# Conditioning shift and scale for the first block: the weighted sum over 1024 inputs on TensorE instead of VectorE

## The chip, the cores and the metric

One core of one Trainium2 chip runs the whole kernel. The metric is device time in microseconds (us), from start to end of one execution. TensorE (PE in the profile; PEld is its weight load, LDWEIGHTS) multiplies a stationary block of up to 128 columns with a moving operand and writes into PSUM. VectorE (DVE), ScalarE (ACT) and GpSimd (POOL) do the elementwise work, and SyncE (SP) issues the DMA transfers.

## What is computed

A decoder layer on 2048 tokens of width 1024. What matters here is its very first part: a vector `c` is put through SiLU and projected to six vectors of 1024; the first two, a shift and a scale, act on the normalised input before its projection.

```python
x = layer_norm(x, ln_in_g, ln_in_b)
c_act = jax.nn.silu(c)
mod = c_act @ w_ada[l] + b_ada[l]
sh1, sc1, gt1, sh2, sc2, gt2 = [m[:, None, :] for m in jnp.split(mod, 6, axis=-1)]
h = x * (1.0 + sc1) + sh1
proj = h @ w_in[l]
```

Behind this stand attention in a low-rank form, a retention mixer, the output projection and a squared-ReLU MLP, all in float32, with the large products computed as three products of split operands.

## The kernel before

The tokens are worked in four blocks of 512 (four tiles of 128 tokens). In the first stage, `ln_in` loads a tile of x (L259) and normalises it: statistics on DVE (L187 to L198) with two small steps on POOL (L179, L180), then the scaling on ACT (L262). `make_h` transposes the normalised tiles on TensorE so that features lie on partitions (L276, eight feature blocks k, four transposes each), applies scale and shift while it takes them out of PSUM (ACT, L280), splits the result in a high and a low part (L124, L126, L127) and stores it for a later stage (L283). `in_proj_mm` then does the first input projection, 416 columns wide, with three matmuls for each pair of token tile and k (L130 to L132, tiles `pa`), 96 for a block.

The shift and scale that L280 needs come from `w_ada`, a matrix of 1024 by 2048 for these two vectors (8 MB). The loop over g at L309 takes it in four groups; group g gives the features of blocks k = 2g and 2g + 1. For each group eight tiles of 128 x 2 x 256 are loaded (L313, tiles `wada`, 256 KB each, 21 buffers under the tag `wt`, later used for other weights too). `cact` holds the activated vector, one column for each of the eight input blocks. DVE then multiplies tile 0 by its column (L324) and adds the seven others, each times its column (L326), into the same tile. What is left is a sum over the 128 partitions, done by TensorE: with the bias put into PSUM first (L329, the identity as stationary operand), four matmuls add it up (L332), with a 128-column piece of the accumulated tile stationary and one column of ones moving. Three small DVE steps make the scale `gs1` and the shift `bs1` out of it (L333 to L335). `make_h(0, ...)` for this group and, for g > 0, the projection of the group before it follow (L336 to L341).

The text of the program is not the order of instructions. A scheduler orders each engine's queue at build time by priorities and a simulated timeline; what stands under `tc.high_priority` (L322 to L335) is preferred as soon as it is ready there. Each engine then works through its queue in that order, and SP issues the transfers in a fixed order as well. PSUM tiles of the tag `tp` (four buffers) serve `psX` and the transposes `psT`, and four of the tag `mm` serve `pa`.

Of the kernel before, what the change touches and what calls it, by code (L numbers as in the profile page):

```python
# [14 lines left out]
OP = mybir.AluOpType  # L15
# [3 lines left out]
P = 128  # L19
# [5 lines left out]
KD = D // P  # L25
# [90 lines left out]
def build(nc, tc, I, out, upto=9, dbg=None):  # L116
    dbg = {} if dbg is None else dbg
    V, A, G, T, Q = nc.vector, nc.scalar, nc.gpsimd, nc.tensor, nc.sync
# [39 lines left out]
    def fmc(n):  # L158
        return fm[:, FM[n][0]:FM[n][1]]
# [6 lines left out]
    ones = keep.tile([P, P], F32, name="ones")  # L166
# [3 lines left out]
    cact = keep.tile([P, 8], F32, name="cact")  # L170
# [67 lines left out]
    def tables16():  # L238
        a16 = s1.tile([P, NT, 16], F32, tag="ang", name="a16")
        V.tensor_tensor(a16, posf.unsqueeze(2).broadcast_to([P, NT, 16]),  # L240
                        cnc("inv16").unsqueeze(1).broadcast_to([P, NT, 16]), op=OP.mult)
        sincos(s1, a16.rearrange("p a b -> p (a b)"), NT * 16, sin16[:, :, 16:32], cos16[:, :, 0:16], "a16")
        G.tensor_copy(cos16[:, :, 16:32], cos16[:, :, 0:16])
        G.tensor_scalar(sin16[:, :, 0:16], sin16[:, :, 16:32], -1.0, 0.0, op0=OP.mult, op1=OP.add)
# [12 lines left out]
    def ln_in(tt):  # L257
        xt = px.tile([P, D], F32, tag="x", name=f"x{tt}")
        Q.dma_start(xt, I["x"][tt * P:(tt + 1) * P, :])  # L259
        rs, nm = xst[:, tt, 0:1], xst[:, tt, 1:2]  # L260
        ln_stats(sm, xt, rs, nm)
        A.activation(xt, xt, AF.Identity, bias=nm, scale=rs)  # L262
        xts[tt] = xt
# [5 lines left out]
    def make_h(b, ks=range(KD)):  # L269
        if ks[0] == 0:  # L270
            hs[b] = hp.tile([P, 4, KD, P], R32, tag="hh", name=f"hh{b}"), hp.tile([P, 4, KD, P], R32, tag="hl", name=f"hl{b}")
        hh, hl = hs[b]
        for k in ks:
            ps = pst1.tile([P, 4, P], F32, tag="tp", name=f"psT{b}_{k}")
            for t in range(4):
                T.transpose(ps[:, t, :], xts[4 * b + t][:, k * P:(k + 1) * P], ident)  # L276
            if k % 2 == 0:
                h2 = hfp.tile([P, 4, 2, P], F32, tag="hf", name=f"hf{b}_{k}")
            hf = h2[:, :, k % 2]
            A.activation(hf, ps, AF.Identity, bias=bs1[:, k:k + 1], scale=gs1[:, k:k + 1])  # L280
            split(hf, hh[:, :, k, :], hl[:, :, k, :], HH[HHE[b > 0]], HH[HLE[k % len(HLE)]] if b == 0 else V)
            if k % 2 == 1:
                Q.dma_start(h_d[b].rearrange("t p k c -> p t k c")[:, :, k - 1:k + 1], h2)  # L283
# [3 lines left out]
    def in_proj_mm(b, order):  # L287
        hh, hl = hs[b]
        for t, k in order:
            if k == 0:  # L290
                pas[b, t] = ps1.tile([P, 512], F32, tag="mm", name=f"pa{4 * b + t}")
            mm3(pas[b, t][:, 0:NA], hh[:, t, k, :], hl[:, t, k, :], wa_h[:, k, :], wa_l[:, k, :], k == 0, k == KD - 1)
# [8 lines left out]
    def load_wa(ks):  # L301
        for k in ks:
            wt = s0.tile([P, NA], F32, tag="wt3", name=f"wa{k}", bufs=6)
            Q.dma_start(wt, I["w_in_a"][k * P:(k + 1) * P, :])
            split(wt, wa_h[:, k, :], wa_l[:, k, :], A, G)
# [3 lines left out]
    for g in range(4):  # L309
        wts = []  # L310
        for k in range(KD):
            wt = s0.tile([P, 2, 256], F32, tag="wt", name=f"wada{g}_{k}", bufs=WTB)
            Q.dma_start(wt, I["w_ada"][k * P:(k + 1) * P, 0:2 * D].rearrange("p (e c) -> p e c", e=2)  # L313
                        [:, :, g * 256:(g + 1) * 256])
            wts.append(wt)
        if g == 0:
            ln_in(2)
            ln_in(3)
            load_wa(range(0, 4))
        if g == 1:  # L320
            load_wa(range(4, 8))
        with tc.high_priority(offset=HPO):  # L322
            acc = wts[0]
            V.tensor_scalar(acc, acc, cact[:, 0:1], None, op0=OP.mult)  # L324
            for k in range(1, KD):
                V.scalar_tensor_tensor(acc, wts[k], cact[:, k:k + 1], acc, op0=OP.mult, op1=OP.add)  # L326
            psA = pst1.tile([P, 2, 2], F32, tag="tp", name=f"psX{g}")
            fs = slice(2 * g, 2 * g + 2)
            T.matmul(psA, ident, fmc("b_ada")[:, 0:16].rearrange("p (s k) -> p s k", s=2)[:, :, fs], start=True, stop=False)  # L329
            for e in range(2):  # L330
                for f in range(2):
                    T.matmul(psA[:, e, f:f + 1], acc[:, e, f * P:(f + 1) * P], ones[:, 0:1], start=False, stop=e + f == 2)  # L332
            V.scalar_tensor_tensor(gs1[:, fs], psA[:, 1, :], 1.0, fmc("gin")[:, fs], op0=OP.add, op1=OP.mult)  # L333
            V.scalar_tensor_tensor(bs1[:, fs], psA[:, 1, :], 1.0, fmc("bin")[:, fs], op0=OP.add, op1=OP.mult)
            V.tensor_tensor(bs1[:, fs], bs1[:, fs], psA[:, 0, :], op=OP.add)  # L335
        make_h(0, [2 * g, 2 * g + 1])  # L336
        if g > 0:
            in_proj_mm(0, [(t, k) for k in (2 * g - 2, 2 * g - 1) for t in range(4)])
        if g == 0:
            tables16()  # L340
# [3 lines left out]
    for k in range(2):  # L344
        for c0, c1 in ((0, 512), (512, WQ)):
# [4 lines left out]
                                   op0=OP.mult, op1=OP.subtract)  # L350
# [810 lines left out]
    acc = {}  # L1161
# [147 lines left out]
def program(L, upto=9, dbg=None):  # L1309
    import concourse.bacc as bacc  # L1310
    nc = bacc.Bacc("TRN2", target_bir_lowering=False, num_devices=1)
    I = {n: nc.dram_tensor(f"in_{n}", v.shape, mybir.dt.from_np(v.dtype), kind="ExternalInput").ap() for n, v in L.items()}
    out = nc.dram_tensor("out", (S, D), F32, kind="ExternalOutput").ap()
    with tile.TileContext(nc, schedule_with_timeline_sim=True) as tc:
        build(nc, tc, I, out, upto, dbg)
    return nc
# [8 lines left out]
```

## Time and profile before

| | us |
|---|---|
| median of 3 runs (lowest, highest) | 2668.42 (2666.13, 2670.19) |
| the profiled execution | 2668.93 |
| its span, first to last instruction | 2667.2 |
| busy PE, PEld | 2461.4, 2030.5 |
| busy DVE, ACT, POOL | 1895.4, 1061.6, 1155.0 |

The busy time of an engine counts its instructions; overlapping ones are counted once. The granted clock (PEclk) is a share of the full rate of TensorE, 1.00 or 0.50. In the trace of this kernel one matmul call in float32 stands as two LDWEIGHTS and two MATMUL, except for transposes. In a timeline, neighbouring instructions of the same kind are merged, with their count behind an x; what stands in brackets is the engine's idle time before them and what ended it.

### The profile page before, as it was taken

How to read it: one execution, taken by the hardware profiler on the slowest of the kernel's cores; microseconds unless marked ns; L12 is line 12 of the kernel's file. 1: busy time of each engine (PE TensorE's matmuls, PEld its weight loads, DVE VectorE, ACT ScalarE, POOL GpSimd, SP SyncE). 2: the span in 40 equal slices, each digit the busy share in tenths (PEclk: the TensorE clock that was granted, in tenths of full speed). 3: DMA queues.
4: the chain of work that ended last, by engine and by line, in shares of the span. 5: the costliest groups of instructions: out<-in, count | busy, mean ns of one | idle time of the engine just before them, and what ended most of it. 6: DMA issues, size and time to landing. Idle time of an engine off the chain costs nothing.

```text
span 2667.2 us, 33679 instructions
## 1 busy us (share of the span) xinstructions
PE 2461.4 (92%) x11668; PEld 2030.5 (76%) x11668; DVE 1895.4 (71%) x3047; ACT 1061.6 (40%) x2093; POOL 1155.0 (43%) x1055
## 2 busy tenths in 40 slices
PE   6999999989999999999689998799998999999996
PEld 5887878877787878787477786577786888878885
DVE  8757675566767676856898877988765665786657
ACT  4653222256777777434433334233321211221111
POOL 4323545557888888587612335432330000330004
PEclk9999999989999999999799999899998999999998
DMA  9466341020102021556487852677739677676653
GB/s 324 145 208 209 115 131 44 32 75 28 58 23 64 22 60 48 184 183 215 147 265 251 283 180 76 218 255 270 278 102 374 257 257 261 257 282 241 230 192 126
DMA packets 194250, 464.68 MB, mean 174 GB/s; under 512 B 17560, under 2 KB 51736, under 8 KB 179744
## 3 DMA queue, kind: packets, MB, share of 16 engines
q1 hardware_dynamic: 194080, 462.54, 50.0%
q8 instruction: 92, 1.51, 0.2%
q14 instruction: 78, 0.64, 0.1%
HBM read 313.30 MB, written 149.17 MB: 173 GB/s over the span
## 4 chain that ended last, share of the span: by engine, by line
PE 53%; DVE 17%; DMA 13%; issue 7%; POOL 6%; ACT 4%; SPq 1%; DVEq 0%; ACTq 0%; POOLq 0%
PE d_W L130 4%; PE d_W L132 4%; PE d_W L131 4%; DMA wt_d<-w2s 4%; PE t L833 3%; DMA wad<-in_w_ada 2%; PE pj L132 2%; PE pj L131 2%; PE pj L130 2%; PE o L826 2%; PE d_Z L130 2%; PE d_Z L131 2%; PE d_Z L132 2%; DVE w1l_P L127 2%; PE o L824 2%
## 5 line engine op out<-in xcount | busy, mean ns | idle before, releaser
L179 POOL TENSOR_SCALAR rs<-mv 128x1 f32<-128x1 f32 x32 | 18.2, 574 | 595.9 <-DVE mv L189 594.2
L124 ACT ACTIVATE w1h_P<-w 128x512 fp32r<-128x512 f32 x224 | 136.7, 625 | 202.9 <-POOL w L1073 96.0
L1073 POOL TENSOR_TENSOR w<-w 128x512 f32<-128x512 f32 x56 | 90.1, 1608 | 288.0 <-DMA w<-in_w_ff 230.6
L800 DVE TENSOR_REDUCE mx<-s 128x1 f32<-128x512 f32 (+3 forms) x288 | 175.1, 620 | 54.5 <-PE s L132 51.8
L805 ACT ACTIVATE p<-s,nm 128x512 f32<-128x512 f32 (+3 forms) x320 | 196.5, 627 | 41.2 <-DVE nm L802 37.7
L127 DVE TENSOR_TENSOR w1l_P<-w,w1h_P 128x512 fp32r<-128x512 f32 x224 | 183.1, 824 | 30.9 <-ACT w1h_P L124 30.3
L849 POOL TENSOR_TENSOR tl<-tf,th 128x512 fp32r<-128x512 f32 x144 | 184.9, 1295 | 1.7
L833 PE MATMUL t<-ident,p 128*128 128x128 f32 x1088 | 164.0, 276 | 5.6 <-ACT tf L844 2.2
L1073 POOL TENSOR_TENSOR w<-w,w 128x512 f32<-128x512 f32 x56 | 92.7, 1656 | 140.8 <-DVE w1l_P L127 140.8
L833 PEld LDWEIGHTS t<-ident,p 128*128 128x128 f32 x1088 | 130.2, 142 | 30.3 <-ACT tf L844 6.3
L124 ACT ACTIVATE w2s<-w2r 128x512 fp32r<-128x512 f32 x112 | 70.5, 630 | 206.7 <-DMA wt_d<-w2s 164.5
L130 PE MATMUL pj<-wbh,hhb 128*128 128x512 f32 x384 | 151.5, 397 | 1.0 <-ACT wbh L124 0.6
L131 PE MATMUL pj<-wbl,hhb 128*128 128x512 f32 x384 | 152.0, 396 | 0.2 <-DVE wbl L127 0.2
L132 PE MATMUL pj<-wbh,hlb 128*128 128x512 f32 x384 | 152.2, 397 | 0.0
L130 PE MATMUL s<-kt,qt 96*128 96x512 f32 (+3 forms) x320 | 129.5, 405 | 12.0 <-ACT p L805 10.2
L826 PE MATMUL o<-tl,v 128*128 128x512 f32 (+2 forms) x320 | 124.0, 396 | 6.4 <-DVE tl L127 4.9
L824 PE MATMUL o<-th,v 128*128 128x512 f32 (+2 forms) x320 | 122.1, 386 | 5.8 <-DVE osum L860 4.7
L132 PE MATMUL u_X<-hh_P,w1l_P 128*128 128x512 f32 x256 | 104.3, 407 | 23.7 <-DVE w1l_P L127 23.7
L131 PE MATMUL s<-kt,qt 96*128 96x512 f32 (+3 forms) x320 | 119.6, 374 | 3.7 <-DVE kt L127 3.7
L132 PE MATMUL s<-kt,qt 96*128 96x512 f32 (+3 forms) x320 | 119.5, 374 | 0.0
L130 PE MATMUL u_W<-hh_P,w1h_P 128*128 128x512 f32 x256 | 102.1, 399 | 12.9 <-ACT hh_P L124 6.7
L1235 DVE TENSOR_TENSOR acc<-acc,d_W 128x512 f32<-128x512 f32 x128 | 85.4, 683 | 40.3 <-PE d_W L132 39.9
(371 smaller groups left out, 7833.3 us busy)
## 6 DMA issues: line engine op xcount, KB each, us to landing
wP<-wt_d SPq DMA_DIRECT2D x112, 1024.0 KB, 4.9
wt_d<-w2s SPq DMA_DIRECT2D x112, 512.0 KB, 3.6
w<-in_w_ff SPq DMA_DIRECT2D x64, 512.0 KB, 4.5
g_d<-r SPq DMA_DIRECT2D x128, 256.0 KB, 3.9
a<-g_d SPq DMA_DIRECT2D x32, 1024.0 KB, 9.1
wad<-in_w_ada SPq DMA_DIRECT2D x64, 256.0 KB, 2.9
w2r<-in_w_ff SPq DMA_DIRECT2D x16, 1024.0 KB, 7.1
x<-in_x SPq DMA_DIRECT2D x16, 512.0 KB, 8.4
```

Of the source, the lines that this page charges most:

```text
L124: A.activation(hi, x, AF.Copy)
L127: lo_eng.tensor_tensor(lo, x, hi.bitcast(F32), op=OP.subtract)
L130: T.matmul(ps, sh, mh, start=start, stop=False, skip_group_check=more)
L131: T.matmul(ps, sh, ml, start=False, stop=False, skip_group_check=more)
L132: T.matmul(ps, sl, mh, start=False, stop=stop, skip_group_check=more)
L800: V.tensor_reduce(mx[:, j:j + 1], ps[:, :n], op=OP.max, axis=AX.X)
L805: A.activation(pt[:, :m], b[:, :m], AF.Exp, bias=nm, accum_out=rs[:, qi, j:j + 1])
L824: T.matmul(po[:, cs], w, th[:, cs], start=(done == 0), stop=False)
L826: T.matmul(po[:, cs], w, tl[:, cs], start=False, stop=(done == nk))
L833: T.transpose(tp[:, qi * P:(qi + 1) * P], pts[h, 4 * qb + qi, kb // 4][1][:, kb % 4 * P:(kb % 4 + 1) * P], ident)
L849: (V if mode == "C" else G).tensor_tensor(tl[:, cs], tf[:, cs], th[:, cs].bitcast(F32), op=OP.subtract)
L1073: (V if half == 0 and c < W1V else G).tensor_tensor(src, *sub, op=op)
```

## The change

The accumulation on DVE goes away. Each of the eight tiles of a group is used as it was loaded: its four pieces of 128 columns are the stationary operands, the moving operand is the matching column of `cact` instead of a column of ones, and the sum over the eight tiles is made in PSUM, in the group of matmuls that the bias opens. The bias matmul, the three DVE steps behind it, the loads and everything else in the text stay as they are.

```diff
         with tc.high_priority(offset=HPO):
-            acc = wts[0]
-            V.tensor_scalar(acc, acc, cact[:, 0:1], None, op0=OP.mult)
-            for k in range(1, KD):
-                V.scalar_tensor_tensor(acc, wts[k], cact[:, k:k + 1], acc, op0=OP.mult, op1=OP.add)
             psA = pst1.tile([P, 2, 2], F32, tag="tp", name=f"psX{g}")
             fs = slice(2 * g, 2 * g + 2)
             T.matmul(psA, ident, fmc("b_ada")[:, 0:16].rearrange("p (s k) -> p s k", s=2)[:, :, fs], start=True, stop=False)
-            for e in range(2):
-                for f in range(2):
-                    T.matmul(psA[:, e, f:f + 1], acc[:, e, f * P:(f + 1) * P], ones[:, 0:1], start=False, stop=e + f == 2)
+            for k in range(KD):
+                for e in range(2):
+                    for f in range(2):
+                        T.matmul(psA[:, e, f:f + 1], wts[k][:, e, f * P:(f + 1) * P], cact[:, k:k + 1], start=False, stop=k == KD - 1 and e + f == 2)
             V.scalar_tensor_tensor(gs1[:, fs], psA[:, 1, :], 1.0, fmc("gin")[:, fs], op0=OP.add, op1=OP.mult)
```

## Rows read from the trace of the kernel before

**Rows 1.** Page, part 1: busy us (share of span) xinstructions of each engine.

```profile
PE 2461.4 (92%) x11668; PEld 2030.5 (76%) x11668; DVE 1895.4 (71%) x3047; ACT 1061.6 (40%) x2093; POOL 1155.0 (43%) x1055
```

**Rows 2.** Stretches: us, busy (count) of PE, PEld, DVE, ACT, POOL; PEclk, DMA, GB/s.

```profile
0.00:9.00 9.00, 0.56 (x2) 0.50 (x2) 3.78 (x10) 1.49 (x2) 1.17 (x11) 1.00 0.70 229
9.00:46.00 37.00, 24.13 (x114) 21.16 (x114) 35.38 (x59) 16.87 (x27) 18.55 (x19) 1.00 1.08 368
46.00:64.00 18.00, 13.70 (x71) 11.67 (x71) 14.91 (x38) 12.97 (x20) 10.71 (x12) 0.97 0.86 309
64.00:80.00 16.00, 9.98 (x41) 8.43 (x40) 16.00 (x49) 12.89 (x34) 10.41 (x17) 0.61 0.69 236
80.00:182.00 102.00, 102.00 (x555) 93.42 (x555) 59.06 (x152) 56.66 (x132) 22.48 (x38) 1.00 0.42 141
```

**Rows 3.** Chain that ended last in 0 to 80 us: shares by line.

```profile
by line: DVE wada L326 22.7%; issue 18.9%; DVE st L187 9.3%; DMA x<-in_x 5.9%; POOL hl L127 4.8%; DVE wada L324 3.7%; PE pa L132 3.1%; POOL xst L180 3.1%; ACT hf L280 2.6%; PE psX L332 2.3%; PE psT L276 2.1%; PE psN L392 1.9%; POOL rr L180 
```

**Rows 4.** DVE by line, 0 to 80 us: busy us, mean ns, idle before.

```profile
L326 DVE SCALAR_TENSOR_TENSOR wada<-wada,cact,wada 128x512 f32<-128x512 f32 x28 | 24.8, 885 | 0.6
L324 DVE TENSOR_SCALAR wada<-wada,cact 128x512 f32<-128x512 f32 x4 | 3.5, 882 | 0.0
```

**Rows 5.** SP's timeline (start us, us, what); landing times of tile wada.

```profile
3.05 5.45 SPq L313 DMA_DIRECT2D wada<-in_w_ada  x8
28.38 5.28 SPq L313 DMA_DIRECT2D wada<-in_w_ada  x8
...
DMA to landing us min/median/max: 5.5/6.0/6.5
```

**Rows 6.** Timeline around the last group and the handover: start, us, engine, line.

```profile
49.81 0.15 DVE L333 SCALAR_TENSOR_TENSOR gs<-psX,fm 128x2 f32<-128x2 f32 x1
...
62.55 1.48 PE L132 MATMUL pa<-wa_h,hl 128*128 128x416 f32 x4 [2.13 <-POOL hl L127]
66.45 0.38 ACT L367 ACTIVATE junk<-pa 128x256 f32<-128x256 f32 x1
68.84 0.37 ACT L373 ACTIVATE qn<-pa,rr 128x128 f32<-128x128 f32 x1
73.79 0.17 DVE L375 TENSOR_TENSOR qn<-pa,cos 128x32 f32<-128x32 f32 x1
75.35 0.70 PE L130 MATMUL pa<-wa_h,hh 128*128 128x416 f32 x1
```

**Rows 7.** Timeline of TensorE: bursts of L332 and loads of the projection.

```profile
27.63 1.78 PEld L332 LDWEIGHTS psX<-ones,wada 128*128 128x128 f32 x8 [0.46 <-DVE wada L326]
...
31.37 0.33 PEld L131 LDWEIGHTS pa<-wa_l,hh 128*128 128x128 f32 x1
31.72 0.33 PEld L130 LDWEIGHTS pa<-wa_h,hh 128*128 128x128 f32 x1
41.18 0.19 PEld L130 LDWEIGHTS pa<-wa_h,hh 128*128 128x128 f32 x1
41.37 0.19 PEld L131 LDWEIGHTS pa<-wa_l,hh 128*128 128x128 f32 x1
45.59 0.97 PEld L332 LDWEIGHTS psX<-ones,wada 128*128 128x128 f32 x8 [0.22 <-DVE wada L326]
```

**Rows 8.** Table by stretch, as above: granted clock (PEclk) around its changes.

```profile
28.00:30.00 2.00, 2.00 (x11) 2.00 (x11) 1.96 (x5) 2.00 (x4) 1.36 (x2) 1.00 1.09 360
31.00:35.00 4.00, 4.00 (x13) 3.80 (x13) 3.93 (x7) 2.12 (x4) 1.18 (x1) 1.00 1.09 348
60.00:63.00 3.00, 0.87 (x5) 0.52 (x4) 1.84 (x4) 2.29 (x4) 3.00 (x2) 0.99 0.41 140
63.00:66.00 3.00, 3.00 (x15) 2.86 (x14) 3.00 (x5) 1.00 (x2) 2.15 (x2) 0.50 0.64 225
67.00:69.00 2.00, 0.00 (x0) 0.00 (x0) 2.00 (x5) 1.97 (x9) 1.26 (x3) 1.00 0.67 135
75.00:79.90 4.90, 4.90 (x18) 4.62 (x17) 4.90 (x21) 3.24 (x5) 4.13 (x7) 0.50 0.60 222
```

## The prediction

> **What bounds the kernel now.** I read from the outside in. Over the whole run TensorE is busy 92% of the span, DVE 71% [rows 1]. The change touches only the start, so the next view is the table by stretch [rows 2]: until 9 us almost nothing runs on TensorE, from 9 to 80 us it has gaps, and from 80 to 182 us it is busy 102.00 of 102.00 us, with DVE and ACT at little more than half. So from 80 us on the kernel is bound by TensorE, and what counts is only how early TensorE reaches the point in its work at which it stood at 80 us. A delay of that point is handed on: behind it stands a full queue.
>
> Inside the first 80 us two other resources look full: DVE has 35.38 of 37 us between 9 and 46, and the DMA share is 1.08 there [rows 2]. The chain that ended last in this stretch is led by the projection on DVE, 22.7% plus 3.7% of 80 us, about 21 us [rows 3]. Taken alone, that view says: take the 28 instructions of L326 (24.8 us) and the 4 of L324 (3.5 us) off DVE [rows 4] and the stage gets shorter. The same stretch has a price on the other side, though, and it is paid on TensorE.
>
> **The idle time of TensorE that the change can use.** Busy time in the first 80 us is 0.56 + 24.13 + 13.70 + 9.98 = 48.4 us [rows 2], so 31.6 us are idle. Not all is usable. The first w_ada tile is issued at 3.05 us and lands after about 6.0, so at 9 us [rows 5]; the 8.4 us before it stay empty. At the handover between the first and the second input projection, the PSUM tiles of the first have to be read before the second can start. Before, this took from the last L132 at 62.55 + 1.48 = 64.03 us to 75.35 us [rows 6], partly because ACT and DVE were behind. The pure chain is shorter: first square to second scaling on ACT, 66.45 to 68.84 + 0.37, is 2.8 us, and three short DVE reads of about 0.17 make it 3.3 us [rows 6]. Usable: 31.6 - 8.4 - 3.3 = about 20 us.
>
> **What is added.** Each group g had four one-column matmuls; in the trace each call is two LDWEIGHTS and two MATMUL, eight pairs a group [rows 7]. The change makes it 32 calls, 64 pairs a group, 256 in all, 224 more. The price of a pair comes from the bursts that exist. Eight loads took 1.78 us at 27.63 us and 0.97 us at 45.59 us [rows 7]; less the last load (0.33 and 0.19 us, as long as the projection's loads near them) and divided by seven, the pitch is 0.207 and 0.111 us. The first burst lies in the slow stretch: the projection's loads, one for each matmul, start 0.35 us apart at 31.37 us and 0.19 us apart at 41.18 us [rows 7], nearly a ratio of two, the two levels of the clock (1.2 and 2.4 GHz). So the added work is 224 x 0.207 = 46.4 us at the low level or 224 x 0.111 = 24.9 us at the high one. Either is more than the 20 us of usable idle time. The moving operand is one column; what is paid for is the loading of 128 weight columns, twice.
>
> The Trainium skill, page "TensorE: Matmul & The Clock Gate", section "LDWEIGHTS (loading the stationary operand)", says that a load takes time by its number of weight columns, P/1.2 ns, whatever streams behind it. That speaks against this change, which loads a fresh block for every single column. By it, an estimate, 224 loads would be 224 x 0.107 = 24 us; the bursts agree at the high level and cost twice that at the low one.
>
> **Which clock level.** This is the one large unknown, since the trace has no long run of one-column matmuls. The clock column reads 1.00 up to 46 us [rows 2, 8], which the pitch contradicts, so up to 35 us I go by the pitch. TensorE was busy 2.00 of 2.00 us from 28 to 30 us, partly with one-column matmuls, and 4.00 of 4.00 from 31 to 35 us with the projection; the pitch was still slow there, and is fast at 41 [rows 7, 8]. At 63 us the granted clock fell to 0.50, after 3 us with 0.87 busy; it rose again once TensorE had run 128- and 416-column matmuls without a gap from 63 to 66 us, and once more after the dense 75 to 79.9 us [rows 8]. Every rise followed a stretch dense with wide matmuls. The new work is the opposite: for a k block 8 x 0.207 = 1.7 us of loads, with eight columns streamed. I take it that this keeps the low level, and that the projection's matmuls, which the scheduler will put between the blocks, run slow with it. Bounds for the 224 pairs are the two figures above; I take 46.4, for the start of the run is slow in any case, and it is there that the first blocks stand.
>
> **The sum.** 46.4 added, less 20 filled into idle time: +26 us. The rest nearly cancels: the input projection's matmuls of 36 to 46 us, fast before, would now lie between slow blocks (10 us less some 3 of transposes and bursts, at 0.19 a matmul, are some 37 of the 96; at +0.16 each +6 us), while the work of 63 to 80 us, slow before (9.98 us busy at a mean clock of 0.61 from 64 on [rows 2]), would follow a dense stretch and get about 5 us shorter. Net I take 25 us, with 18 to 34 as its own range (idle time that doesn't get filled, or projection matmuls moved behind all blocks).
>
> **What costs nothing, and its cover.** DVE loses 28.3 us of work [rows 4]; TensorE, not DVE, then ends the stage, so this gives only the faster handover counted above, plus the 3 us by which L333 of the last group, at 49.81 us [rows 6], came after the end of its burst at 45.59 + 0.97 [rows 7], queued on DVE behind other work. The transfers stay as they are: the 32 loads are issued up to 28.38 + 5.28 us [rows 5]. They wait for one of 21 buffers, now freed by TensorE instead of DVE; the last one needs the eleventh tile, done at about 9 + 11 x 1.7 = 27 us even in the slow case. Behind them on SP stand the loads of x for the next block, so 0 here, and if blocks came 6 us later these loads would slip by as much, hidden behind TensorE's queue. The new matmuls wait for transfers in TensorE's own in-order queue, where transposes and the projection stand behind them; at 1.7 us a block against 0.66 us an issue TensorE is the later one, so these waits cost little beyond the first block. psX holds one of four PSUM buffers for 8 x 1.7 = 13 us; the transposes have the others: 0, bounded by 0 and 3 us.
>
> **The rivals.** *Partly fast.* If the projection's matmuls between the blocks of the last two groups are dense enough, the clock rises there: 128 pairs at 0.111 save 128 x 0.096 = 12 us, so +13 us, 5 to 18. For it: three such matmuls (0.19 or 0.35 us each) could stand between two blocks. Against it: a mix without a gap stayed slow from 28 us to 35 [rows 8].
>
> *Fast from the start, ending not slower.* If loading weights by itself raises the clock, the added work is 24.9 us, 5 more than the idle time, and the slow stretches of before turn fast: 64 to 80 us alone gives back 5 us, the stretch before 35 us a few more. That gives 0, from -9 to +3. The -9 would need TensorE to keep up with the transfers: the last tile lands at 33.7 + 6.0 = 39.7 us [rows 5], six before the last burst starts now [rows 7], and L333 need not queue for 3 us. It decides by whether the level is high when group 2 starts, near 27 us. For it: TensorE would be busy nearly without gaps from 9 us on, where before it was idle for 13 of the 37 us to 46 [rows 2]. Against it: the busy stretch with one-column work at 28 us, which stayed slow [rows 7, 8].
>
> The Trainium skill, same page, section "Part 1: The HAM clock gate", states that the default is the throttled level and that sustained activity releases it. If loads count as activity, that rule gives this rival's 0; no row here shows a run of loads that settles it, which is why the rival has a fifth of the chance.
>
> **How the numbers follow.** The profiled execution took 2668.93 us, 1.73 more than its span, and stands 0.5 over the median of the three runs. 2668.9 + 25 = 2694 us. Chances: slow throughout 0.55 (2687 to 2703), partly fast 0.20 (2674 to 2687), fast 0.20 (2660 to 2672), anything else, such as another order of instructions later in the run, 0.05. A measurement of this kernel tells about 0.2%, 5.3 us, from no change. Slower by more than that: the first two and half of the last, 0.76; within it 0.15, most of the fast case; faster 0.09, the end of it. The range reaches from 2666, which takes in nearly half of the fast case, to 2703.
>
> **What would show it.** In the profile after: 256 pairs for psX with a mean start distance near 0.21 us; the granted clock or the pitch low until the last of them; the first input projection ending near 90 us instead of 64; TensorE's solid stretch shifted by about 25 us and everything later with it; DVE far from full before 46 us. If the pitch is near 0.11 us from 20 us on and the second projection starts by 76 us, the clock step is wrong. If TensorE stands idle waiting for w_ada between blocks, the order step is wrong. If the stretch shifts but the end doesn't, the claim that delay is handed on is wrong.

## The result, and the profile after

The change makes the kernel slower: 2685.49 us median of 8 runs (2679.49 to 2692.86) against 2666.62 us of 8 runs of the kernel before (2662.67 to 2672.01), a ratio of 1.0069 with a 95% interval of 1.0054 to 1.0084. That is +18.9 us, with 14 to 22 as the interval, where 25 were predicted with 18 to 34 as the likeliest case's own range. The profiled execution took 2685.27 us, its span 2683.5.

Part 1 of the page after answers to [rows 1]: busy us (share of the span) and instructions of each engine.

```profile
PE 2503.6 (93%) x11892; PEld 2077.1 (77%) x11892; DVE 1872.1 (70%) x3015; ACT 1061.8 (40%) x2093; POOL 1146.0 (43%) x1055
```

TensorE has 224 pairs and 42.2 us of busy time more; DVE has 32 instructions and 23.3 us less. The table by stretch shows where this stands; its columns are those of [rows 2].

```profile
0.00:9.00 9.00, 1.03 (x5) 1.01 (x5) 4.45 (x12) 1.49 (x2) 1.69 (x11) 1.00 0.71 226
9.00:46.00 37.00, 37.00 (x177) 37.00 (x176) 12.44 (x36) 16.14 (x24) 16.12 (x23) 1.00 1.08 368
46.00:64.00 18.00, 18.00 (x93) 17.70 (x93) 11.97 (x31) 9.62 (x14) 4.90 (x6) 1.00 0.32 112
64.00:80.00 16.00, 16.00 (x82) 15.70 (x82) 2.77 (x7) 2.72 (x4) 1.27 (x1) 0.68 0.12 37
80.00:100.00 20.00, 17.63 (x90) 15.70 (x89) 14.09 (x35) 15.12 (x34) 8.00 (x15) 0.83 0.73 239
```

From 9 to 46 us DVE fell from 35.38 us [rows 2] to 12.44, and TensorE rose from 24.13 to 37.00: the full engine has changed. After 9 us TensorE has no idle time before 80 us. The timeline of TensorE around the sum, with columns as in [rows 6 and 7]:

```profile
8.52 13.78 PE L329 MATMUL psX<-cact,wada 128*128 128x1 f32 x64 [5.31 <-DMA wada<-in_w_ada]
23.37 13.65 PE L329 MATMUL psX<-cact,wada 128*128 128x1 f32 x64
39.77 13.79 PE L329 MATMUL psX<-cact,wada 128*128 128x1 f32 x64
53.42 0.69 PE L130 MATMUL pa<-wa_h,hh 128*128 128x416 f32 x1
53.91 0.55 PE L131 MATMUL pa<-wa_l,hh 128*128 128x416 f32 x1
59.20 0.35 PE L132 MATMUL pa<-wa_h,hl 128*128 128x416 f32 x1
61.20 9.69 PE L329 MATMUL psX<-cact,wada 128*128 128x1 f32 x64
71.29 0.69 PE L130 MATMUL pa<-wa_h,hh 128*128 128x416 f32 x1
76.15 0.35 PE L132 MATMUL pa<-wa_h,hl 128*128 128x416 f32 x1
88.26 0.35 PE L132 MATMUL pa<-wa_h,hl 128*128 128x416 f32 x1
96.07 0.72 PE L130 MATMUL pa<-wa_h,hh 128*128 128x416 f32 x1
```

The 64 pairs of a group run as one block. In the first three groups a pair takes 13.7/64 = 0.214 us, the price of the slow burst in [rows 7]. The first projection begins at 53.42 us; its last matmul ends at 88.6 us, against 64.03 before [rows 6], and the second starts at 96.07, against 75.35.

The chain that ended last in 0 to 100 us, by line, which answers to [rows 3]:

```profile
by line: PE psX L329 50.4%; DMA x<-in_x 6.9%; PE pa L130 6.5%; PE psT L276 5.9%; PE pa L131 5.7%; PE pa L132 5.5%; DMA wada<-in_w_ada 5.3%; issue 4.3%; SPq L259 1.3%; ACT x L262 1.2%; ACT hf L280 1.0%; ACT junk L364 0.9%; DVE st L187 0.7%; 
```

The sum held about 21 us of the chain on DVE; it holds 50 us of it on TensorE now.

**A ledger of the front.** To compare many kernels I use one point, the end of the input projection's last matmul over all four blocks (the end of the front), and split the time up to it: idle TensorE, the matmuls of the sum (`psX`), and the rest. All figures are in us, summed from the matmul records of one profiled execution each; where two matmuls overlap, the time counts for the earlier one. "Order" says whether TensorE's 10,848 matmuls behind the front, from the retention mixer's first one on, stand in the same order as in the kernel before (A), in that of the kernel after (B), or in another (other); the scheduler sets it anew for each kernel. The psX of swap has its row matmuls in it, that of the warm kernels the wide matmuls between the blocks (the 15 at their start stand in the rest).

| kernel | end of front | idle | psX | first projection ends | second starts | order | median against before |
|---|---|---|---|---|---|---|---|
| before | 171.1 | 31.6 | 6.9 | 64.0 | 75.4 | A | |
| after | 192.3 | 10.3 | 51.5 | 88.6 | 96.1 | B | +18.9 |
| nosum | 165.7 | 26.9 | 6.0 | 46.9 | 67.3 | other | -1.3 |
| noload | 147.6 | 13.2 | 8.7 | 47.2 | 51.1 | other | -9.7 |
| both | 193.9 | 11.9 | 51.6 | 89.8 | 97.9 | B | +22.2 |
| split2 | 172.4 | 23.8 | 18.1 | 68.8 | 75.6 | A | +2.4 |
| split4 | 181.2 | 19.5 | 30.7 | 75.8 | 80.6 | other | +7.6 |
| warm2 | 215.8 | 6.7 | 74.5 | 112.1 | 120.1 | other | +50 |
| warm1 | 202.3 | 7.0 | 60.3 | 98.5 | 106.4 | other | +40 |
| warm5 | 201.8 | 6.1 | 65.6 | 96.9 | 104.8 | other | +41 |
| prio0 | 196.7 | 9.2 | 40.4 | 98.0 | 101.6 | other | +34 |
| swap | 180.7 | 18.0 | 35.3 | 74.1 | 85.4 | other | +16 |
| earlyx | 170.6 | 32.6 | 7.0 | 66.1 | 76.4 | other | +6.7 |
| splitx | 166.4 | 19.4 | 16.6 | 63.2 | 70.0 | B | -12.2 |

For the change: psX +44.6, idle -21.3, the rest -2.1, together +21.2 at the end of the front.

### The profile page after: what moved, and what is told of

The parts are those of the page before. It is cut to its first block, busy times and chain, and to the rows that moved or that the text cites. A ratio compares the mean times of both kernels' runs of the same rounds, so it can differ in the third digit from the quotient of the medians.

```text
span 2683.5 us, 34080 instructions
## 1 busy us (share of the span) xinstructions
PE 2503.6 (93%) x11892; PEld 2077.1 (77%) x11892; DVE 1872.1 (70%) x3015; ACT 1061.8 (40%) x2093; POOL 1146.0 (43%) x1055
## 4 chain that ended last, share of the span: by engine, by line
PE 54%; DVE 17%; DMA 13%; issue 6%; POOL 4%; ACT 4%; SPq 1%; DVEq 0%; ACTq 0%; POOLq 0%
PE d_W L130 4%; PE d_W L132 4%; PE d_W L131 4%; DMA wt_d<-w2s 4%; PE t L830 3%; DMA wad<-in_w_ada 2%; PE pj L132 2%; PE pj L130 2%; PE pj L131 2%; PE d_Z L132 2%; PE d_Z L130 2%; PE o L823 2%; PE d_Z L131 2%; PE s L130 2%; PE psX L329 2%
## 5 line engine op out<-in xcount | busy, mean ns | idle before, releaser
L130 PE MATMUL s<-kt,qt 96*128 96x512 f32 (+3 forms) x320 | 129.3, 404 | 12.9 <-ACT p L802 9.4
L131 PE MATMUL s<-kt,qt 96*128 96x512 f32 (+3 forms) x320 | 120.1, 375 | 3.7 <-DVE kt L127 3.7
L132 PE MATMUL u_X<-hh_P,w1l_P 128*128 128x512 f32 x256 | 105.6, 412 | 14.9 <-DVE w1l_P L127 14.9
L127 DVE TENSOR_TENSOR w2s<-w2r,w2s 128x512 fp32r<-128x512 f32 x112 | 88.8, 795 | 41.9 <-ACT w2s L124 41.4
L130 PE MATMUL u_Z<-hh_P,w1h_P 128*128 128x512 f32 x256 | 104.7, 409 | 10.8 <-ACT w1h_P L124 7.8
```

The costliest lines, as they stand in the source:

```text
L127: lo_eng.tensor_tensor(lo, x, hi.bitcast(F32), op=OP.subtract)
L130: T.matmul(ps, sh, mh, start=start, stop=False, skip_group_check=more)
L131: T.matmul(ps, sh, ml, start=False, stop=False, skip_group_check=more)
L132: T.matmul(ps, sl, mh, start=False, stop=stop, skip_group_check=more)
```

## The experiments

**Is the sum on DVE worth taking away at all?** Before any price is paid on TensorE, `nosum` removes the accumulation and pays nothing. It leaves out seven eighths of the sum: only tile 0 is used.

```diff
-            V.tensor_scalar(acc, acc, cact[:, 0:1], None, op0=OP.mult)
-            for k in range(1, KD):
-                V.scalar_tensor_tensor(acc, wts[k], cact[:, k:k + 1], acc, op0=OP.mult, op1=OP.add)
```

> The kernel before without the accumulation over the eight tiles: only the first tile of each group goes into the four one-column matmuls, so neither VectorE nor TensorE does the sum (that part of the projection is left out). It shows what taking the 28 us off VectorE is worth when TensorE gets nothing in exchange. Theory (VectorE's sum was the chain of the first 64 us, the time then falls on the transfers): 5 to 9 us faster than before. Rival (the first stage is bound by the transfers, DMA share 1.08, and the sum was hidden): within 2 us of before.

Measured: 2666.73 us against 2668.07, ratio 0.9992 (0.9983 to 1.0001); the front ends 5.4 us earlier. The first projection ended 17 us earlier, at 46.9 us, and yet the second started only 8 us earlier. From nosum's timelines, SP's issues of x for the second block and TensorE's start on it, and from its chain that ended last in 40 to 70 us the line by line (the x transfer in it begins at 34.40 us):

```profile
34.40 1.82 SPq L259 DMA_DIRECT2D x<-in_x  x2
37.36 1.00 SPq L259 DMA_DIRECT2D x<-in_x  x2
...
67.27 0.71 PE L130 MATMUL pa<-wa_h,hh 128*128 128x416 f32 x1 [1.92 <-DVE tk L374]
...
by line: DMA x<-in_x 25.2%; DVE st L187 22.2%; DVE pri L210 10.2%; DMA pri<-in_pos_row 9.4%; DVE hh L126 6.7%; DVE k_T L207 6.1%; DVE hl L127 6.0%; issue 5.1%; PE pa L130 4.7%; DVE posfb L511 3.8%; DVE pri L251 2.7%; PE pa L132 2.3%; PE pa 
```

The x tiles of the second block are issued behind all loads of `w_ada`, and the first lands at 41.99 us. From there to 67.27 us the chain is mostly DVE: it normalises x, splits `hh` and `hl`, makes tables (`pri`, `k_T`), and only behind that comes to `tk` L374, the read of the first projection's result that the second projection waits for. So even free relief of DVE is worth 5.4 us in the front and nothing that can be measured at the end: the theory of a 5 to 9 us faster kernel falls. The number of its rival, the transfers, holds; its reason holds in part, since the sum was not hidden in the first projection, which ended 17 us earlier without it. For the front as a whole the chain that was led by the sum [rows 3] has others close behind it.

`noload` also leaves out the loads of tiles 1 to 7, again without seven eighths of the sum.

```diff
-        for k in range(KD):
+        for k in range(1):
             wt = s0.tile([P, 2, 256], F32, tag="wt", name=f"wada{g}_{k}", bufs=WTB)
```

> The kernel before without the accumulation on DVE and without the loads of tiles 1 to 7 of each group; only tile 0 stands in for the sum, so seven eighths of the projection are left out. Loads of w_ada: 4 instead of 32, which frees about 28 x 0.66 = 18 us of SP's issuing ahead of x of the second block. Question: does time gained in the first 165 us reach the end of the run? Theory (the transfers of the start bound it, and a gain is handed on as a delay is): the first input projection over all four blocks ends 13 to 23 us earlier than the 171.1 us of before, its TensorE idle time is down from 31.6 to under 18 us, and the end is 8 to 20 us faster than before. Rival (later work waits for something that does not move with the front, such as loads issued at a fixed pace or DVE): the front is shorter by as much, but the end is within 4 us of before; then the 5 us that were gained in front without the sum alone, and lost later, are of the same kind, and only delays are handed on.

Measured: 2656.82 us against 2666.56, ratio 0.9955 (0.9938 to 0.9971). The front ends 23.5 us earlier, with 13.2 us idle: the theory's figures, the first just past its edge. With the sum gone, the transfers bound the start: the second projection begins 16.2 us earlier than in nosum (51.09 against 67.27 us), which differs in the loads alone. No run leaves out loads and keeps the sum. At the end 9.7 of the 23.5 us are left (6.7 in the profiled execution); the order of later matmuls differs in 1621 of 10,848 places, which is taken up below.

**Does TensorE lose by the pairs, or by something that DVE no longer does?** `both` is the kernel after with the accumulation kept on DVE as well, its result unused.

```diff
+            acc = s0.tile([P, 2, 256], F32, tag="accx", name=f"accx{g}", bufs=2)
+            V.tensor_scalar(acc, wts[0], cact[:, 0:1], None, op0=OP.mult)
+            for k in range(1, KD):
+                V.scalar_tensor_tensor(acc, wts[k], cact[:, k:k + 1], acc, op0=OP.mult, op1=OP.add)
```

> The changed kernel with VectorE's accumulation kept beside TensorE's sum, in a spare tile that nobody reads. Theory (TensorE ends the stage in the changed kernel, so VectorE's 28 us are hidden there): the changed kernel's time within 2 us, so about 19 us over before. Rival (the relief of VectorE gave back a part of the cost in the changed kernel): 25 to 28 us over before.

Measured: 2690.29 us, ratio to before 1.0081 (1.0067 to 1.0095): +22.2, which lies between the two expectations. Against the kernel after, the front ends 1.6 us later and the end comes 4.8 us later. Taken against the kernel before that ran beside each, the end comes 3.3 us later. 28 us of DVE work cost 2 to 5 us: TensorE, not DVE, ends the stage after the change.

**The price in steps.** `split2` and `split4` give TensorE the last two or four of the eight tiles; DVE adds up the others (diff for two).

```diff
-            for k in range(1, KD):
+            for k in range(1, KD - 2):
...
-            for e in range(2):
-                for f in range(2):
-                    T.matmul(psA[:, e, f:f + 1], acc[:, e, f * P:(f + 1) * P], ones[:, 0:1], start=False, stop=e + f == 2)
+            for w, col in [(wts[k], cact[:, k:k + 1]) for k in range(KD - 2, KD)] + [(acc, ones[:, 0:1])]:
+                for e in range(2):
+                    for f in range(2):
+                        T.matmul(psA[:, e, f:f + 1], w[:, e, f * P:(f + 1) * P], col, start=False, stop=w is acc and e + f == 2)
```

> VectorE sums six tiles of a group, TensorE adds the last two itself: 24 pairs a group instead of 8 (before) or 64 (changed), so 64 more than before in all. Theory (a ledger: about 20 us of idle time in TensorE's start swallow 64 x 0.214 = 13.7 us): 4 us faster to 2 us slower than before, and VectorE's sum 7 us shorter. Rival (every pair costs alike, 18.9 us for 224): 5.4 us slower than before.

> As the one with two tiles, but with four of eight on TensorE: 40 pairs a group, 128 more than before. Theory (ledger): 128 x 0.214 = 27.4 less some 20 of idle time, 3 to 8 us slower than before. Rival (every pair costs alike): 10.8 us slower. If idle time is not used at all: 27 us slower.

Measured: +2.4 us (ratio 1.0006, 0.9997 to 1.0015) and +7.6 us (1.0029, 1.0019 to 1.0039). In the front the steps are +1.4, +10.1 and, for all eight tiles, +21.2 us. The ledger shows why it isn't a straight line: of the 11.2, 23.8 and 44.6 us added, idle time takes 7.8, 12.1 and 21.3. The ledger's bounds hold for four tiles and are missed by 0.4 us for two; the straight line (5.4 and 10.8 us) lies outside both intervals. Of the first pairs idle time covers two thirds, of all of them half. No split is faster than none.

**Can the clock be bought?** `warm2` puts 15 matmuls of 512 columns ahead of everything and 2 of 508 columns in front of each k block of eight pairs, all into unused PSUM columns; `warm1` and `warm5` have 1 and 5 in front of each block.

```diff
+    with tc.high_priority(offset=2 * HPO):
+        psW = pst1.tile([P, 512], F32, tag="tp", name="psW")
+        for i in range(15):
+            T.matmul(psW, wide[:, 0:P], wide, start=True, stop=True)
...
             for k in range(KD):
+                for i in range(2):
+                    T.matmul(psB[:, 4:512], wide[:, 0:P], wide[:, 0:508], start=False, stop=False, skip_group_check=True)
```

> The changed kernel with extra wide matmuls whose results nobody reads: 15 of 512 columns on TensorE before the first w_ada tile lands, and two of 508 columns ahead of each block of eight pairs. Theory (the new work is dear because it runs at the low clock level, 0.214 us a pair instead of 0.111): the pitch of the pairs falls to 0.11 us, a block with its two wide ones takes about 0.89 + 2 x 0.21 = 1.3 us instead of 1.7, the sum is done 12 us earlier although there is more work, and the time is 2 to 9 us over before instead of 19. Rival (the low level has another cause, such as the start of the run): the pitch stays at 0.21, the extra work costs 64 x 0.42 = 27 us more, 40 us or more over before.

> As the one with two wide matmuls per block, with one. Theory (one of 508 columns in each block is enough to hold the level): a block takes 0.89 + 0.21 = 1.1 us, 0 to 6 us over before, and faster than the one with two. If one is not enough: the level falls during the first group, blocks take 1.71 + 0.42 = 2.1 us, and the time is 25 to 35 us over before.

> As the one with two wide matmuls ahead of each block (in which the level fell to the low one at 14 us and stayed there), but with five: 96 wide matmuls more. Theory (the level decides, and this denser mixture holds it): a block takes 0.89 + 5 x 0.21 = 1.95 us where the one with two took 2.55, so more work takes less time: the sum ends near 75 us instead of 94.6, and the whole is 25 to 35 us over before, against 50 with two. Rival (the level doesn't hold, or the low pitch isn't due to it): a block takes 1.71 + 5 x 0.42 = 3.8 us, 85 to 95 us over before.

Measured: 2715.3 us (ratio 1.0181, 1.0164 to 1.0197), 2705.2 (1.0147, 1.0125 to 1.0169) and 2710.85 (1.0152, 1.0125 to 1.0179). The level fell in warm1 and warm2 (0.50 in warm1 from 20 to 60 us) and held in warm5. First warm2: its table by stretch and, from TensorE's timeline, a block ahead of the fall and one behind it.

```profile
9.00:14.00 5.00, 4.97 (x38) 4.69 (x38) 1.72 (x7) 3.49 (x5) 1.91 (x5) 0.98 1.09 369
14.00:20.00 6.00, 6.00 (x24) 5.54 (x25) 2.89 (x7) 2.65 (x5) 3.06 (x6) 0.50 1.06 370
20.00:40.00 20.00, 20.00 (x82) 18.63 (x80) 2.76 (x9) 3.90 (x7) 7.83 (x10) 0.50 1.08 367
...
10.51 0.95 PE L340 MATMUL psX<-cact,wada 128*128 128x1 f32 x8
16.81 1.19 PE L337 MATMUL psX<-wide 128*128 128x508 f32 x2
17.81 1.70 PE L340 MATMUL psX<-cact,wada 128*128 128x1 f32 x8
```

Then warm5, the same two views:

```profile
9.00:14.00 5.00, 5.00 (x32) 4.45 (x32) 0.79 (x5) 3.50 (x5) 1.60 (x4) 1.00 1.08 374
14.00:20.00 6.00, 6.00 (x40) 5.46 (x39) 2.89 (x7) 3.12 (x5) 3.42 (x6) 1.00 1.06 366
20.00:40.00 20.00, 20.00 (x134) 18.16 (x133) 4.66 (x13) 5.11 (x8) 7.51 (x10) 1.00 1.08 368
...
17.03 1.38 PE L337 MATMUL psX<-wide 128*128 128x508 f32 x5
18.24 0.95 PE L340 MATMUL psX<-cact,wada 128*128 128x1 f32 x8
```

In these rows TensorE is busy for all but 0.03 us. With two wide matmuls a block the granted clock is 0.50 from 14 us to 75 us, behind the first three groups; with five it stays at 1.00 up to 80 us. Eight pairs take 1.70 us in the one and 0.95 in the other. So the premise for warm2, that two would hold the level, was wrong, and its time came out at the rival's 40 us or more. The rival's reason was wrong too: the low level isn't tied to the start of the run, since warm2 began at the high one. warm5 issues 96 wide matmuls more than warm2, and its front still ends 14 us earlier: so the level is worth more than those 96. It is no way out: the five wide matmuls cost 1.2 us a block and give back 0.75. The size was missed as well: the sum of warm5 ended at 81.6 us, not near 75, and its +41 us lie 6 above the range of 25 to 35; the +40 of warm1 lie 5 above its own. The ends of the three can't be set against each other, since their later order differs (warm5 from warm2 in 612 places).

**Would projection matmuls between the pairs raise the level?** `prio0` sets the offset of the priority to 0, so that the scheduler mixes the sum with the projection.

```diff
-HPO = 600
+HPO = 0
```

> The changed kernel without the raised priority of the sum (the priority offset 0 instead of 600): the scheduler then puts, in two of the four groups, about one matmul of the input projection between two calls of the sum, instead of 64 pairs in one run. Theory 1 (the amount of TensorE's work decides and the mixture stays at the low level): 15 to 23 us over before, as the changed kernel. Theory 2 (the mixture holds the high level; the partly fast case of the prediction): two groups run at 0.111 us a pair, 10 to 13 us less than the changed kernel, 5 to 10 us over before.

Measured: 2699.24 us against 2665.07, ratio 1.0132 (1.0105 to 1.0159). A piece of its timeline, and the stretch around it:

```profile
41.97 0.69 PE L132 MATMUL pa<-wa_h,hl 128*128 128x416 f32 x1
42.46 0.42 PE L329 MATMUL psX<-cact,wada 128*128 128x1 f32 x2
42.74 0.69 PE L130 MATMUL pa<-wa_h,hh 128*128 128x416 f32 x1
43.23 0.42 PE L329 MATMUL psX<-cact,wada 128*128 128x1 f32 x2
...
40.00:60.00 20.00, 20.00 (x84) 19.69 (x84) 15.93 (x41) 11.80 (x17) 9.28 (x10) 1.00 0.60 206
```

One projection matmul and one call of two pairs take 0.77 us together, both at the price of the low level: the loads of the projection start 0.35 us apart in [rows 7] and a slow call is 0.43. Mixed in this way the projection's matmuls are slow as well (95.3 us of busy time for `pa` instead of 77.8), and the kernel is dearer than the change itself, by 4.4 us in the front and 15 at the end. Its +34 us miss both theories (15 to 23, 5 to 10); why, against the change, the end lost 11 us more than the front is open; prio0 has an order of its own. The column of the granted clock still reads 1.00 here; the pitch says otherwise, as it did in the kernel before.

**The other way round.** `swap` makes the column of `cact` stationary and lets the tile stream, 512 columns wide, into one row of PSUM; DVE copies the row, and four one-column matmuls turn it.

```diff
-                for e in range(2):
-                    for f in range(2):
-                        T.matmul(psA[:, e, f:f + 1], wts[k][:, e, f * P:(f + 1) * P], cact[:, k:k + 1], start=False, stop=k == KD - 1 and e + f == 2)
+                T.matmul(psR[0:1, :], cact[:, k:k + 1], wts[k].rearrange("p e c -> p (e c)"), start=k == 0, stop=k == KD - 1)
```

> The changed kernel with the operands of the sum exchanged: the activated vector is stationary (one column) and the weights move, 512 columns a tile, into one row of PSUM; VectorE copies the row, and four one-column matmuls a group turn it onto the partitions, as in the kernel before. One float32 call of 512 columns takes about 0.86 us at the high level (two in the trace of before, 1.02 us, less the 0.16 by which the last one's end lies behind the next start), so the 32 calls take 27.5 us at the high level, the same as the 128 one-column calls would. Theory (what makes the changed kernel dear is that its matmuls stream one column and so lose the high level): these calls stream wide, the level rises early in the sum, and the time is 3 to 10 us over before, 9 to 16 less than the changed kernel. Rival (any sum on TensorE of this amount is equally dear): 15 to 23 us over before.

Measured: 2686.57 us against 2670.23, ratio 1.0062 (1.0037 to 1.0086). The front ends at 180.7 us, 11.6 before that of the change and 9.6 behind that of before. Two of the runs of its sum, the first half of the first group and the third group:

```profile
8.00 5.22 PE L328 MATMUL psRow<-wada,cact 128*1 128x512 f32 x8 [4.70 <-DMA wada<-in_w_ada]
...
34.47 7.03 PE L328 MATMUL psRow<-wada,cact 128*1 128x512 f32 x16
```

At the high level a tile costs 7.03/8 = 0.88 us this way, against 8 x 0.111 = 0.89 with the blocks stationary: two instructions of 512 columns are as dear as eight pairs. What this form gains is the level: from 34 us a group takes 7.03 us, where the kernel after has 13.8 us for its third one. The expectation of 3 to 10 us held at the front (+9.6) and failed at the end (+16, within the rival's 15 to 23; +11 in the profiled execution); the later order is another one too, so the end doesn't decide between the two.

**A version that is faster.** nosum suggested that x of the second block comes late. `earlyx` is the kernel before with those loads and their normalisation ahead of the last group; `splitx` is split2 with the same move.

```diff
+        if g == 2:
+            for t in range(4, 8):
+                ln_in(t)
...
-    for t in range(4, 8):
-        ln_in(t)
```

> The kernel before, whole, with the four x tiles of the second block loaded and normalised ahead of the last group of w_ada instead of behind it (the text of lines 342 and 343 is moved into the loop, at g = 2). It asks whether the handover between the first and the second projection (64.03 to 75.35 us in the profile of before) waits for x, as the run without the sum suggested. Theory (x of the second block comes too late): x is issued some 6 us earlier, the second projection starts 5 us after the first at most, the projections over all blocks end at 163 to 168 us instead of 171.1, the end is 2 to 8 us faster. Rival (DVE is full until 64 us, so work brought forward pushes the sum back): the first projection ends some 7 us later, the projections over all blocks end at 170 to 175 us, the end is within 3 us of before.

> The same move of the x tiles in the kernel in which TensorE takes the last two of the eight tiles of each group (+2.4 us so far). Theory (with two tiles off DVE there is room for the normalisation of the second block): the projections over all blocks end at 163 to 169 us against 172.5 without the move and 171.1 before, and the end is 1 to 8 us faster than before. Rival (the added pairs on TensorE cost their price wherever x stands): the projections end at 171 to 175 us, the end 0 to 5 us slower than before.

Measured: earlyx 2676.02 us against 2669.28, ratio 1.0031 (1.0019 to 1.0043); splitx 2657.05, ratio 0.9953 (0.9936 to 0.9969). With the whole sum on DVE the move gains nothing: the burst of the last group comes at 54.68 us instead of 45.59 [rows 7], and the front ends within 0.5 us of before, the rival's case, though the first projection ends 2 us later and not 7, and the end is 4 us past the bound of 3. With two tiles off DVE it pays, as the theory had it: the second projection starts at 70.0 us and the front ends at 166.4; the end is 4 us beyond the theory's bound. splitx is 12.2 us faster than the kernel before and 28.4 us faster than the change. Only 4.7 of the 12.2 us lie in the front; where the other 7.5 come from no run shows.

**Is a delay in front handed on?** This is the prediction's claim from [rows 2]. Kernels with the same order behind the front answer it:

| pair, same order | end of front | first matmul of the retention mixer | end of output in the trace | medians |
|---|---|---|---|---|
| split2 less before (A) | +1.4 | +1.5 | +2.1 | +2.4 |
| both less after (B) | +1.6 | +3.0 | +5.5 | +4.8 |
| after less splitx (B) | +25.9 | +25.0 | +29.2 | +28.4 |

With the same order all of it is handed on in these pairs, and a little more (the last two medians, taken against the kernel before that ran beside each, are +3.3 and +31.1). Between orders the traces agree less: after less before is +21.2 at the front and +16.3 at the end of output, splitx less before -4.7 and -12.9, noload less before -23.5 and -6.7. Each is one execution, though, and the eight of the kernel before lie up to 9 us apart. For the change the medians decide, and +18.9 with its interval of 14 to 22 takes in the 21.2 of the front: that some of the delay was lost is not shown.

Where the two traces lose 5 us can be read all the same. The kernel after lags by 21.2 us at the end of the front, by 20.1 at the mixer's first matmul (220.62 against 200.47 us), by 19.0 at 16 one-column matmuls named `psG`, by 17.4 behind them (347.53 against 330.16), and by 16.2 at the MLP's first `u_W` matmul. Orders A and B differ in 471 of 10,848 places, the first of them near 580 us, so most of this happens with the order still the same. The matmuls `psG`, a wide one behind them, and the stretch that follows, first in the kernel before and then in the kernel after:

```profile
323.82 1.84 PE L554 MATMUL psG<-ones,acc 128*128 128x1 f32 x16
326.35 0.63 PE L130 MATMUL pj<-wbh,hhb 128*128 128x512 f32 x1
326.00:329.00 3.00, 3.00 (x9) 2.35 (x8) 1.18 (x3) 0.26 (x1) 2.34 (x4) 0.50 0.64 211
...
342.78 1.84 PE L551 MATMUL psG<-ones,acc 128*128 128x1 f32 x16
345.03 0.39 PE L130 MATMUL pj<-wbh,hhb 128*128 128x512 f32 x1
345.00:348.00 3.00, 3.00 (x17) 2.46 (x16) 1.13 (x3) 0.31 (x1) 2.30 (x4) 1.00 0.65 215
```

The same matmuls stand in both, but the granted clock fell to 0.50 in the kernel before and not in the kernel after, which gave the kernel after 1.6 us. The largest step between the two orders is at the start of the MLP, the first quarter of the up projection's `u_W` matmuls. That stretch in the kernel before, the kernel after and splitx, in this order:

```profile
1303.44:1500.14 196.70, 170.03 (x705) 135.62 (x706) 176.34 (x230) 77.63 (x130) 53.81 (x27) 0.93 0.79 256
```

```profile
1319.66:1509.26 189.60, 169.49 (x705) 136.28 (x706) 175.37 (x228) 76.59 (x128) 49.90 (x27) 0.93 0.77 259
```

```profile
1294.63:1485.63 191.00, 171.98 (x705) 138.57 (x706) 176.30 (x228) 76.78 (x128) 48.92 (x27) 0.92 0.76 258
```

TensorE has the same work in it, 170 to 172 us, but 26.7 us of idle time in order A and 20.1 or 19.0 in order B. `both` (B) takes 190.2 us there, nosum, which has the order of B in this stretch, 189, and split2 (A) 196.4. So order B reaches the end of this stretch some 6 us sooner, whatever the front does. It is no gain at the end of the kernel: the kernel after is 9.1 us behind where the stretch ends (1509.26 against 1500.14 us), but 14.9 again at 1533 us of the kernel before and 16.3 at the end of output. No kernel changed this order alone.

## Why the prediction was right, point by point

**What bounds the start.** Right. From 9 us on TensorE is full and DVE is not, and nosum and both confirm that relief of DVE is worth little in the front, 5.4 us in the one and 1.6 in the other. The chain's 26% for the sum would have misled.

**The pairs.** 46.4 us were predicted for 224 pairs, 44.6 measured. The price at the low level was 0.214 us instead of 0.207. Not all pairs ran at it: the last group began at the high level and took 9.69 us instead of 13.7.

**The clock step.** Right in its result, with a wrong detail: no projection matmuls stood between the blocks. The scheduler ran 64 pairs in one go, and in the first three groups, 13.7 us each without a gap, the pitch stayed that of the low level. That shows the rival "fast from the start" wrong, and the fourth group tells more. The table by stretch after, with the granted clock (third number from the end):

```profile
61.00:64.00 3.00, 3.00 (x31) 3.00 (x28) 1.96 (x5) 1.41 (x2) 0.00 (x0) 1.00 0.06 21
64.00:66.00 2.00, 2.00 (x19) 2.00 (x19) 1.93 (x3) 0.00 (x0) 0.00 (x0) 0.93 0.00 0
66.00:70.00 4.00, 4.00 (x20) 4.00 (x20) 0.46 (x2) 0.00 (x0) 0.00 (x0) 0.50 0.00 0
71.00:75.00 4.00, 4.00 (x14) 3.83 (x14) 0.31 (x3) 1.41 (x2) 1.27 (x1) 0.50 0.38 131
76.00:80.00 4.00, 4.00 (x26) 3.91 (x25) 0.00 (x0) 1.31 (x2) 0.00 (x0) 1.00 0.11 18
```

The projection ahead of it had raised the level. Within the run of pairs it fell to 0.50 while TensorE was busy 2.00 of 2.00 and then 4.00 of 4.00 us, and it rose again only behind the projection's matmuls that follow from 71.29 us.

The Trainium skill, "TensorE: Matmul & The Clock Gate", section "Part 1: The HAM clock gate", says that activity releases the throttle. If activity is what the profile counts as busy time, these rows differ: TensorE was never idle, and the clock fell. The measurement decides.

**Partly fast.** The price of that rival rested on projection matmuls between the blocks. prio0 made such a mixture, one projection matmul for every two pairs, and from 40 us to 47 it stayed slow; its front ended 4.4 us later than that of the change. One part of the rival came in by another way: the projection between the third and the fourth group raised the level, and the last group took 4 us less than the others. The median of 2685.49 us lies in this rival's bracket (2674 to 2687) and not in that of slow throughout (2687 to 2703). By the difference it is the other way round: +18.9 us lies just over this rival's 5 to 18 and inside 18 to 34. So the number alone doesn't tell the two cases apart; the pitch of the first three groups does.

**The idle time.** About 20 us were to be filled, 21.3 were. The parts are right too: 10.3 us stay idle, against 8.4 + 3.3 = 11.7, most of it ahead of the first tile at 8.52 us and 2.4 in the handover from 80 to 100 us. The time from the last matmul of the first projection to the first of the second is 7.5 us and not 3.3, but transposes fill most of it.

**The rest of the front.** Taken as +1, measured -2.1. The projection's matmuls cost 1.3 us more (+6 expected, since they were to lie among slow blocks, which they didn't), and transposes and `psN` 3.3 less. So the front moved by 21.2 us where 25 were predicted: 1.8 from the pairs, 1.3 from the idle time and 3.1 from the rest, less 2.4 by which the prediction's own terms, 46.4 - 20 + 6 - 5 = 27.4, stand above the 25 that it took. It gives no reason for taking less; that this brought the number nearer is luck. Its chances for slower, 0.55 + 0.20 + half of 0.05, make 0.775 and not 0.76.

**Handed on.** Right for the change, as far as the medians tell: 21.2 us at the front, 18.9 at the end with 14 to 22 as the interval. It is no general rule. The prediction named another order of instructions only as its last 0.05 and gave it no price, and the scheduler made another order in 12 of the 13 other kernels. By the medians front and end differ by 4 to 14 us, in either direction, in three kernels with an order of their own (nosum, earlyx, noload) and in splitx, which is as much as many an edit in the front is worth. What makes up these differences is open.

## What to carry to other kernels

A matrix times one column had no cheap form on TensorE here, in float32: a tile of 128 x 512 took 0.89 us at the high level and 1.71 at the low one with its blocks stationary, and 0.88 with the vector stationary, where DVE's step took 0.885 on average [rows 4]. Before such a price is paid, a kernel with the step left out says what can be won at all (5 us in the front here, for 45 us of new work). The line that leads the chain of waits may have a close second; taking part of it away (two tiles of eight) and moving the loads of the next stage forward won 4.7 us in the front, where the one alone lost 1.4 and the other alone won 0.5. When a scheduler orders the queues, an edit at the start changes the order elsewhere: compare kernels at a point close to the edit, and don't explain a few us at the end by one stretch before it is clear that they last to the end.

## What was not expected of the hardware

The granted clock fell from 1.00 to 0.50 near 66 us in the kernel after while TensorE was busy without a gap, with nothing but one-column matmuls and their loads. After 15 matmuls of 512 columns at the start of warm2 and warm5 the level was high; it fell at 14 us in warm2, with 2 of 508 columns ahead of every eight pairs, and stayed high in warm5, with 5. Behind the same 16 one-column matmuls `psG` the granted clock fell in the kernel before (0.50 from 326 to 329 us) and not in the kernel after. The pitch of a pair follows the level, 0.214 and 0.111 us, so a load of 128 weight columns has no fixed time here. And the column of the granted clock reads 1.00 over the first groups of the kernel after, where the pitch of 0.214 us shows the low level.
